# Hidden tiles turned only behind two-target products, and a down block's sums split in two

## The chip, the cores and the metric

One core of one Trainium2 chip runs the whole layer. The metric is the device time of one execution in microseconds (us); the runs of one kernel lie within a few tenths of a per cent of each other. Every time below comes from one profiled execution unless the text says that it is a median of runs.

## The reference, cut to what matters

The layer takes x of 256 tokens by 2048 columns in float32. It is a SwiGLU feed-forward network (FFN), a token mixer, and a second FFN, with RMS norms between:

```python
def swiglu_ffn(x, w_gate, w_up, w_down):              # 2048 -> 5632 -> 2048
    return (jax.nn.silu(x @ w_gate) * (x @ w_up)) @ w_down

x = x + 0.5 * swiglu_ffn(rms_norm(x, ffn1_norm), ...)
x = x + mixer(rms_norm(x, mix_norm))                  # Hawk recurrence beside a short gated convolution
x = x + 0.5 * swiglu_ffn(rms_norm(x, ffn2_norm), ...)
return rms_norm(x, final_norm)
```

The change touches only the two FFNs, and in them the step from `silu(gate) * up` to the product with `w_down`.

## The kernel before, in words

**Precision.** Every float32 weight tile is split on the chip into a rounded part `hi` (ScalarE, ACT: a cast) and the rest `lo` (VectorE, DVE: a subtraction), both in the format fp32r. A product sums hi·hi, hi·lo and lo·hi. One weight tile (`unit`) is 512 rows by 512 columns, 1 MB, held as 128 x 2048; its split costs two casts of 128 x 1024 and one DVE subtraction of 128 x 2048. The split parts rotate through three sets of buffers, so that the splitting runs about two products ahead of TensorE (PE) and no further.

**Two kinds of product.** `multiply` gets a list of targets (PSUM banks). With one target it issues 12 matmuls of 512 columns, with two targets 24. Inside `seven`, a 2 x 2 block product done in seven multiplications in place of eight (Strassen's scheme, in Winograd's form), the seven products have one target each and need a DVE sum or difference of weight tiles first; the up to four `usual` products between them have two targets. In `down`, the units of `add_units` have two targets, except the last ones of the last block. The order in `seven` is: product 0, product 4, usual, product 5, usual, product 6, product 2, usual, product 3, usual, product 1. The text speaks of them as p0, p4 and so on.

**Stages of an FFN.** The first 512 of the 5632 hidden columns are made plainly (unit 0). Then five rounds s = 0 to 4 follow, each a `seven` on `w_gate` and a `seven` on `w_up`, which give two more hidden units (1+2s and 2+2s) of 512 columns for both halves t = 0, 1 of the tokens. After rounds 0, 2 and 4 comes `down`, which multiplies the units made so far by `w_down`: for output columns 0 and 3 in units of two targets, and for columns 1 and 2 by a `seven` over the last two units m and n. In a down block with `others` the older units, the order is (0, others), (0, n), (3, others), (0, m), then the `seven`, then column 3 of n and m.

**Turning the hidden tiles.** A finished tile `h` has tokens on the partitions and must get its hidden columns there. `part` lets ACT sort the 2-byte halves of h into a buffer `plane` (two of them exist) and has SyncE (SP) issue a transposing DMA from `plane` back to h. `join` lets ACT sort the halves back into `plane`, cast them to the hi part of the big tile `hidden`, and lets DVE subtract for the lo part; in rounds 0, 2 and 4 (`again`) ACT also copies the float32 values to h once more. In the trace these are `COPY plane<-u_g`, `DMA_TRANSPOSE u_g<-plane`, `CAST h<-plane`, `TENSOR_TENSOR h<-plane,h` (with `z`, `s_g`, `sg` in the place of `u_g` for other tiles). A round finishes its four tiles in this order: unit 2+2s with t = 1 and t = 0 (after p6 and p2 of the up `seven`), unit 1+2s with t = 1 and t = 0 (before and after p1).

**When.** A tile is parted as soon as it is queued (`turn_hidden`, `begin_some`) when fewer than two are on the way. After every product of any kind the hook `onward` (in the list `after_product`) counts, joins the tile whose count has reached three, and starts another.

**The sums of a down block.** Its `seven` needs four sums of the float32 tiles of m and n, each split into hi and lo (`seven_of`; in the trace `hspare` and `hs`). `block_sums` makes them all after the unit (0, m) and ahead of the `seven`. The first sum, `spare`, is what p4 uses; `adds` and the rest give what p5, p6 and p2 use.

**What sets the order on an engine.** The kernel is written with a framework that plans the engines' queues while it builds the program. An instruction's place in the program text is its priority; where the planner reckons that its inputs or its buffer are not ready yet, it puts a later instruction that is ready in front. On the chip each engine then works through its own queue in that fixed order. Only `begin` and the end of the last block (`Engine.pinned`) are kept in program order.

Of the kernel before, what the change touches and what calls it, by code (L numbers as in the profile page):

```python
# [21 lines left out]
NT = S // P  # L22
KD = D // P
KF = FF // P
CW = 512
# [24 lines left out]
def hybrid_block(ctx: ExitStack, tc: tile.TileContext, a: dict, out: bass.AP):  # L50
# [35 lines left out]
    def f32(ap):  # L86
        return ap.bitcast(F32)
# [110 lines left out]
    after_product = []  # L198

    def multiply(targets, blk, apart=False, middle=None):  # L200


        more = dict(skip_group_check=True) if apart else {}
        for ps, st, begin, _ in targets:
            for j in range(UK):
                pe.matmul(ps, st[j][0], blk[j][0], start=begin and j == 0, stop=False, **more)
                pe.matmul(ps, st[j][1], blk[j][0], start=False, stop=False, **more)
        if middle:
            middle()
        for ps, st, _, end in targets:  # L210
            for j in range(UK):
                pe.matmul(ps, st[j][0], blk[j][1], start=False, stop=end and j == UK - 1, **more)
        for fn in after_product:
            fn()


    class Norm:
# [93 lines left out]
    def seven_of(sf, x0, x1, v, spare, parts, steps=None):  # L311

        a11, a12, a21, a22 = v[0, 0], v[0, 1], v[1, 0], v[1, 1]
        parts = iter(parts)

        def split(i, q):
            hi, lo = next(parts)
            act.copy(hi, q)  # L320
            dve.tensor_tensor(lo, q, f32(hi), op=ALU.subtract)
            sf[i] = [(hi[:, j, :], lo[:, j, :]) for j in range(UK)]

        sf.update({0: stationary(x0, 0), 1: stationary(x1, 0), 3: stationary(x1, 1)})
        dve.tensor_tensor(spare, a21, a22, op=ALU.add)
        split(4, spare)

        def adds():
            dve.tensor_tensor(a21, a11, a21, op=ALU.subtract)
            dve.tensor_tensor(a11, spare, a11, op=ALU.subtract)  # L330

        def rest():
            if steps is None:
                adds()
            split(5, a11)
            split(6, a21)
# [72 lines left out]
    def ffn(tag, norm, after, opening=False):  # L409
        with (  # L410
# [5 lines left out]
            wg, wu, wd = (a[f"ffn{tag}_w_{s}"][0] for s in ("gate", "up", "down"))  # L416
# [7 lines left out]
            hidden = {}  # L424
# [3 lines left out]
            tiles, moving = deque(), deque()  # L428

            def part(u, t, h, again):  # L430
                two = plane()
                act.copy(two.bitcast(U16).rearrange(flat, b=2), h.bitcast(U16).rearrange(mixed, b=2))
                nc.sync.dma_start(
                    h.bitcast(U16).rearrange("p (r c) -> p r c", c=P), two.bitcast(U16), transpose=True
                )
                return two
# [13 lines left out]

            def turn_hidden(*tile):
                tiles.append(tile)
                begin_some()

            def begin_some():
                while tiles and len(moving) < 2:
                    tile = tiles.popleft()
                    moving.append([0, tile, part(*tile)])

            def onward():  # L460

                for entry in moving:
                    entry[0] += 1
                while moving and moving[0][0] >= 3:
                    _, tile, two = moving.popleft()
                    join(two, *tile)
                begin_some()

            def on_the_way():
                return [*tiles, *(entry[1] for entry in moving)]  # L470

            after_product.append(onward)

            units, vs, sf, ready = [], {}, {}, []

# [200 lines left out]
            def down(last):  # L676
# [40 lines left out]

                def add(t, b, ps, tiles):
                    got[t, b] = [ps] + tiles
# [42 lines left out]
                if s % 2 == 0:  # L762
                    down(s == 4)
            extra.clear()
            after_product.clear()


    def small(name):
# [337 lines left out]
```

## Time and profile before

| | us |
|---|---|
| runs of the kernel | 1749.2, 1751.09, 1754.36 (median 1751.09) |
| the profiled execution, own time | 1749.34 |
| its span from first to last instruction | 1747.3 |
| PE busy in the span | 1710.1 |
| DVE busy | 1486.1 |
| ACT busy | 1137.4 |
| mean granted TensorE clock | 0.997 |

The span is 2.04 us shorter than the execution's own time; the rest lies around it. PE, the engine of the matmuls, is busy for all but 37.2 us of the span. DVE and ACT feed it: where a row shows PE idle, the row's bracket names the instruction of another engine that ended the wait. The names are those of the program with buffer numbers left out: `hi_d_p` and `lo_d_p` are the split parts for a one-target product of a down block's `seven`, `hi_d_x` those of a `usual` one, `raw_d` a weight tile (or, written by DVE, a difference of two), `s_d` a copy of a PSUM bank, `ps_d_c` the bank c of that `seven`; `g`, `u` in the place of `d` mean the gate and up products. Nearly all lines read L43, since one helper records every instruction; the groups are told apart by these names.

### The profile page before, as it was taken

To read this page: it belongs to the slowest core of one execution; us is meant where nothing else is said; L and a number is where in the kernel's file an instruction comes from. 1 tells how busy PE (TensorE), PEld (TensorE's weight loads), DVE (VectorE), ACT (ScalarE), POOL (GpSimd) and SP (SyncE) were. 2 spreads that over 40 slices of the span, in tenths; PEclk is the share of its full clock that TensorE was granted. 3 is DMA by queue.
4 is the path that set the end of the run, shared out by engine and by line. 5 is a ranking of instruction groups with operands and counts; after the bars stand their busy time and mean duration, and the time that the engine had idled before them with its cause. 6 is when DMAs were issued, how large, how long until landed. Compare 5 with 4: busy or idle time off the path is not lost. (4 is left out here: it accounts for less than half of the span.)

```text
span 1747.3 us, 20171 instructions
## 1 busy us (share of the span) xinstructions
PE 1710.1 (98%) x7859; PEld 1417.5 (81%) x7859; DVE 1486.1 (85%) x1233; ACT 1137.4 (65%) x1433; POOL 6.9 (0%) x32
## 2 busy tenths in 40 slices
PE   8999999999999999999999999999999999999998
PEld 6887887888887887888888887787787888878876
DVE  7998999989899888687987668989899888889876
ACT  6767567685567676666665456675567764676854
POOL 1000000000000000000000000000000000000000
PEclk9999999999999999999999999999999999999999
DMA  8566566695567674555556564595476656576852
GB/s 299 195 219 178 206 217 201 208 289 178 184 213 203 216 235 169 193 169 193 170 192 225 191 212 132 194 288 171 172 234 218 205 181 217 192 211 204 265 177 107
DMA packets 220383, 354.75 MB, mean 203 GB/s; under 512 B 52100, under 2 KB 54528, under 8 KB 220160
## 3 DMA queue, kind: packets, MB, share of 16 engines
q1 hardware_dynamic: 219824, 352.36, 62.0%
q8 instruction: 61, 1.00, 0.2%
q10 hardware_dynamic: 144, 1.05, 0.1%
q14 instruction: 34, 0.28, 0.0%
q0 software_dynamic: 320, 0.07, 0.0%
HBM read 339.82 MB, written 2.10 MB: 196 GB/s over the span
## 5 line engine op out<-in xcount | busy, mean ns | idle before, releaser
L43 DVE TENSOR_TENSOR lo_u_p<-raw_u,hi_u_p 128x2048 fp32r<-128x2048 f32 x70 | 159.2, 2286 | 24.4 <-ACT hi_u_p L43 23.9
L43 ACT CAST hi_u_p<-raw_u 128x1024 fp32r<-128x1024 f32 x140 | 141.1, 1047 | 55.5 <-DVE raw_u L43 23.5
L43 ACT CAST hi_g_p<-raw_g 128x1024 fp32r<-128x1024 f32 x132 | 132.9, 1047 | 65.5 <-DVE raw_g L43 40.0
L43 DVE TENSOR_TENSOR lo_g_p<-raw_g,hi_g_p 128x2048 fp32r<-128x2048 f32 x66 | 149.8, 2285 | 30.1 <-ACT hi_g_p L43 30.1
L43 PE MATMUL ps_d<-hi_d,h 128*128 128x512 f32 x704 | 167.2, 389 | 0.0
L43 PEld LDWEIGHTS ps_d<-hi_d,h 128*128 128x128 f32 x704 | 132.1, 188 | 27.4
L43 PE MATMUL ps_in<-xT_nm,hi_in 128*128 128x512 f32 x640 | 153.8, 391 | 0.0
L43 PEld LDWEIGHTS ps_in<-xT_nm,hi_in 128*128 128x128 f32 x640 | 117.2, 188 | 22.9 <-ACT tha L43 0.3
L43 ACT CAST hi_d_p<-raw_d 128x1024 fp32r<-128x1024 f32 x84 | 85.4, 1047 | 74.6 <-DVE raw_d L43 36.4
L43 ACT CAST hi_in<-raw_in 128x1024 fp32r<-128x1024 f32 x80 | 80.1, 1046 | 65.8 <-PE ps_in L43 42.8
L43 DVE TENSOR_TENSOR lo_in<-raw_in,hi_in 128x2048 fp32r<-128x2048 f32 x40 | 91.3, 2284 | 34.8 <-ACT hi_in L43 34.6
L43 DVE TENSOR_TENSOR lo_d<-raw_d,hi_d 128x2048 fp32r<-128x2048 f32 x44 | 100.7, 2289 | 21.1 <-ACT hi_d L43 19.8
L43 ACT CAST hi_u_x<-raw_u 128x1024 fp32r<-128x1024 f32 x80 | 80.4, 1047 | 42.8 <-PE ps_u_c L43 19.7
L43 DVE TENSOR_TENSOR lo_d_p<-raw_d,hi_d_p 128x2048 fp32r<-128x2048 f32 x42 | 95.5, 2285 | 9.3 <-ACT hi_d_p L43 9.2
L43 ACT CAST hi_d<-raw_d 128x1024 fp32r<-128x1024 f32 x88 | 87.9, 1045 | 21.1 <-PE ps_d_d L43 10.1
L43 DVE TENSOR_TENSOR raw_u<-raw_u,raw_u 128x2048 f32<-128x2048 f32 x40 | 91.6, 2290 | 9.6 <-DMA raw_u<-in_ffn_w_up_dram 8.9
L43 ACT CAST hi_g_x<-raw_g 128x1024 fp32r<-128x1024 f32 x80 | 80.2, 1046 | 25.6 <-PE ps_g_c L43 8.6
L43 DVE TENSOR_TENSOR lo_g_x<-raw_g,hi_g_x 128x2048 fp32r<-128x2048 f32 x40 | 91.3, 2284 | 1.6 <-ACT hi_g_x L43 1.5
L43 DVE TENSOR_TENSOR lo_u_x<-raw_u,hi_u_x 128x2048 fp32r<-128x2048 f32 x40 | 91.4, 2284 | 0.3
L43 DVE TENSOR_TENSOR raw_g<-raw_g,raw_g 128x2048 f32<-128x2048 f32 x37 | 84.5, 2285 | 6.0 <-DMA raw_g<-in_ffn_w_gate_dram 5.7
L43 PE MATMUL ps_d<-lo_d,h 128*128 128x512 f32 x352 | 87.3, 389 | 0.0
L43 PEld LDWEIGHTS ps_in<-xT_nm,lo_in 128*128 128x128 f32 x640 | 82.2, 191 | 3.2
(387 smaller groups left out, 3665.2 us busy)
## 6 DMA issues: line engine op xcount, KB each, us to landing
raw_d<-in_ffn_w_down_dram SPq DMA_DIRECT2D x88, 1024.0 KB, 5.6
raw_u<-in_ffn_w_up_dram SPq DMA_DIRECT2D x87, 1024.0 KB, 5.3
raw_g<-in_ffn_w_gate_dram SPq DMA_DIRECT2D x86, 1024.0 KB, 5.4
raw_in<-in_w_in_dram SPq DMA_DIRECT2D x40, 1024.0 KB, 5.1
raw_o<-in_w_out_dram SPq DMA_DIRECT2D x16, 1024.0 KB, 5.1
xres<-in_x_dram SPq DMA_DIRECT2D x4, 512.0 KB, 7.6
raw_u<-in_ffn_w_up_dram SPq DMA_DIRECT2D x2, 512.0 KB, 9.4
raw_g_first<-in_ffn_w_gate_dram SPq DMA_DIRECT2D x1, 1024.0 KB, 12.1
```

The costliest lines, as they stand in the source:

```text
L43: ins = getattr(self.engine, name)(*args, **kwargs)
```

## The change

The hook now runs only after a `multiply` with two targets, and at each such place it does one join and one part: it joins the tile that was parted at the place before, then parts the next in the queue. A tile isn't parted any more when it is queued, and at most one is on the way. Two-target products are the units of `add_units` (but not the very last, which are done one target at a time) and also the `usual` products inside `seven`.

In `down`, the first part of `seven_of` (`spare` and its split) now stands at the first unit after which no tile is on the way, which is ahead of the unit (0, m); the rest (`adds`, three splits, one more difference) stands inside the `seven`, after p4 and its bank copy and ahead of the first usual product.

```diff
-        for fn in after_product:
-            fn()
+        if len(targets) == NT:
+            for fn in after_plain:
+                fn()
...
             def turn_hidden(*tile):
                 tiles.append(tile)
-                begin_some()
-
-            def begin_some():
-                while tiles and len(moving) < 2:
+
+            def onward():
+
+                if moving:
+                    tile, two = moving.popleft()
+                    join(two, *tile)
+                if tiles:
                     tile = tiles.popleft()
-                    moving.append([0, tile, part(*tile)])
-
-            def onward():
-
-                for entry in moving:
-                    entry[0] += 1
-                while moving and moving[0][0] >= 3:
-                    _, tile, two = moving.popleft()
-                    join(two, *tile)
-                begin_some()
+                    moving.append((tile, part(*tile)))
...
-                sh, got = {}, {}
+                sh, got, rest = {}, {}, []
 
                 def block_sums():
-                    seven_of(
+                    return seven_of(
...
-                    )()
+                    )
...
-                for c, u in [(0, u) for u in others + [n]] + [(3, u) for u in others] + [(0, m)]:
+                for c, u in [(0, u) for u in others + [n]] + [(3, u) for u in others]:
                     add_units(c, [u])
-                block_sums()
+                    if not on_the_way() and not rest:
+                        rest.append(block_sums())
+                add_units(0, [m])
                 if tag == 1 and m == 5:
                     prepare()
-                seven(wd, (m, n), (2 * CW, CW), sh, [(u, hidden[u]) for u in others], f"d{tag}_{m}", keep, add)
+                seven(
+                    wd, (m, n), (2 * CW, CW), sh, [(u, hidden[u]) for u in others], f"d{tag}_{m}", keep, add,
+                    lambda i: rest.pop()() if rest else None,
+                )
```

Worked out from the two texts, a tile's places move like this. In rounds 1 and 3, which no down block follows, the second tile of unit 2+2s was joined after the third product behind its start, the fourth usual product of the up `seven`; it is now parted there and joined after the first usual product of the next gate `seven`. The two tiles of unit 1+2s were parted as soon as there was room; they are now parted after the first and second usual products of that gate `seven` and joined after the second and third. In rounds 0, 2 and 4 the down block's first three units take the places of those usual products; there the joins of the two tiles of unit 1+2s stand in the text where they stood before, after the second and the third unit.

More of the change, by code (lines that the diff above doesn't have):

```diff
@@ L196, in stationary @@
         return [(tile[:, j, t * P : (t + 1) * P], tile[:, j, S + t * P : S + (t + 1) * P]) for j in range(UK)]
-    after_product = []
+    after_plain = []
     def multiply(targets, blk, apart=False, middle=None):
@@ L452, in turn_hidden @@
                 tiles.append(tile)
-                begin_some()
-            def begin_some():
-                while tiles and len(moving) < 2:
-                    tile = tiles.popleft()
-                    moving.append([0, tile, part(*tile)])
-            def onward():
-                for entry in moving:
-                    entry[0] += 1
-                while moving and moving[0][0] >= 3:
-                    _, tile, two = moving.popleft()
-                    join(two, *tile)
-                begin_some()
+            def onward():
[3 more added lines that the diff above has]
+                if tiles:
+                    tile = tiles.popleft()
+                    moving.append((tile, part(*tile)))
             def on_the_way():
-                return [*tiles, *(entry[1] for entry in moving)]
-            after_product.append(onward)
+                return [*tiles, *(entry[0] for entry in moving)]
+            after_plain.append(onward)
             units, vs, sf, ready = [], {}, {}, []
@@ L764, in ffn @@
             extra.clear()
-            after_product.clear()
+            after_plain.clear()
     def small(name):
```

## The prediction

> **What bounds the kernel now.** I read the page's first part, then the chain of work that ended last, then the waits of PE, then the busy time by stretch, and last the timeline of one stretch of each kind.
>
> ```profile
> span 1747.3 us, 20171 instructions
> PE 1710.1 (98%) x7859; PEld 1417.5 (81%) x7859; DVE 1486.1 (85%) x1233; ACT 1137.4 (65%) x1433; POOL 6.9 (0%) x32
> ...
> 1259.82 5.44 PE ps_g_a L43 x24
> ...
> PE ps_d_c L43 <- ACT s_d L43: 4.5, 3, 3.0
> PE ps_d_c L43 <- DVE lo_d_p L43: 3.6, 2, 2.4
> ```
>
> PE is the bound: undisturbed it issues 24 matmuls in 5.44 us, 0.227 us each. The change removes no matmul, so all that it can win is PE's idle time, 1747.3 - 1710.1 = 37.2 us. The two longest waits say where much of that is: at the bank c of a down `seven`, that is at p4 and the first usual product; p4 is the first to need a weight difference. In the next table the difference between a stretch and its PE time is the idle time; the first six stretches are beginnings of gate `seven`s, the last six beginnings of down `seven`s.
>
> ```profile
> core 0: us, PE busy (x) PEld busy (x) DVE busy (x) ACT busy (x) POOL busy (x), PEclk, DMA share, GB/s
> 60.00:72.00 12.00, 11.35 (x49) 8.65 (x48) 11.19 (x9) 12.00 (x15) 0.00 (x0) 1.00 0.50 131
> 284.00:299.00 15.00, 13.44 (x58) 10.23 (x58) 14.30 (x12) 13.89 (x16) 0.00 (x0) 1.00 0.41 104
> 535.00:550.00 15.00, 12.68 (x53) 9.43 (x52) 13.28 (x11) 13.62 (x15) 0.00 (x0) 1.00 0.42 111
> 1084.00:1099.00 15.00, 13.06 (x55) 9.59 (x54) 12.86 (x10) 14.56 (x18) 0.00 (x0) 1.00 0.29 81
> 1302.00:1325.00 23.00, 20.81 (x90) 16.15 (x89) 18.78 (x14) 19.16 (x22) 0.00 (x0) 1.00 0.65 156
> 1556.00:1584.00 28.00, 24.90 (x107) 19.54 (x106) 23.41 (x16) 22.16 (x25) 0.00 (x0) 1.00 0.61 151
> 162.00:183.00 21.00, 18.58 (x81) 14.73 (x81) 21.00 (x13) 15.29 (x17) 0.00 (x0) 1.00 0.36 114
> 398.00:419.00 21.00, 21.00 (x94) 17.16 (x94) 20.62 (x28) 13.66 (x17) 0.00 (x0) 1.00 0.21 70
> 655.00:676.00 21.00, 19.70 (x87) 15.96 (x86) 16.86 (x10) 12.92 (x19) 0.00 (x0) 1.00 0.29 101
> 1182.00:1204.00 22.00, 20.53 (x90) 16.23 (x89) 22.00 (x17) 15.78 (x20) 0.00 (x0) 1.00 0.30 96
> 1430.00:1451.00 21.00, 20.80 (x92) 16.89 (x91) 17.53 (x10) 11.89 (x14) 0.00 (x0) 1.00 0.45 151
> 1682.00:1703.00 21.00, 18.01 (x72) 14.39 (x71) 17.05 (x12) 12.79 (x18) 0.00 (x0) 0.92 0.36 117
> ```
>
> Seams into rounds 2 and 4 (284, 535, 1302, 1556): 1.56 + 2.32 + 2.19 + 3.10 = 9.17 us. Round 0 (60, 1084): 0.65 + 1.94 = 2.59 us. Down `seven`s: 2.42 + 0 + 1.30 + 1.47 + 0.20 + 2.99 = 8.38 us. Together 20.1 us; the other 17 us are outside the reach of this change (start, end, mixer, other seams).
>
> **Term 1, the four seams.** One of them in full; the columns are start, duration, engine, and in brackets the idle time before and what ended it.
>
> ```profile
> 1552.60 0.37 SPq L168 DMA_DIRECT2D raw_g<-in_ffn_w_gate_dram  x1
> 1554.29 1.24 SPq L433 DMA_TRANSPOSE u_g<-plane  x1
> 1560.92 0.68 DVE L43 TENSOR_TENSOR z<-ps_u_a,z 128x512 f32<-128x512 f32 x1
> 1562.05 1.35 ACT L43 COPY plane<-u_g 128x1024 uint16<-128x1024 uint16 x1 [3.46 <-DMA u_g<-plane]
> 1563.96 1.04 ACT L43 COPY plane<-z 128x1024 uint16<-128x1024 uint16 x1
> 1564.08 0.69 DVE L43 TENSOR_TENSOR h<-plane,h 128x512 fp32r<-128x512 f32 x1 [2.48 <-ACT h L43]
> 1564.69 2.29 DVE L43 TENSOR_TENSOR raw_g<-raw_g,raw_g 128x2048 f32<-128x2048 f32 x1
> 1564.90 1.99 ACT L43 CAST hi_g_x<-raw_g 128x1024 fp32r<-128x1024 f32 x2
> 1567.01 1.99 ACT L43 CAST hi_g_p<-raw_g 128x1024 fp32r<-128x1024 f32 x2
> 1568.11 2.13 PE L43 MATMUL ps_g_c<-hi_g_p,xs 128*128 128x512 f32 x8 [1.54 <-ACT hi_g_p L43]
> ```
>
> The transposing DMA of the second tile lands at 1562.05, 7.8 us after it was issued. ACT stands 3.46 us before the join that it feeds, DVE 2.48 us before the join's subtraction, and only then come the weight difference for p4 (1564.69), its casts (1567.01) and PE, 1.54 us late; the rest of the stretch's 3.10 us follows behind it.
>
> After the change this join stands in the text behind the first usual product, and so behind the difference and the casts of p4; the next tile's part (1.04 us) likewise. What ACT has ready meanwhile is little, because the three sets of split buffers hold its casts back, so I leave the join in its place on ACT, with its wait. On DVE the difference is ready at 1560.92 + 0.68 = 1561.6, 3.1 us earlier than 1564.69, and is no longer behind the subtraction. On ACT the casts of p4 then start at 1563.96, where the part stood, or after the two casts of `hi_g_x` at 1565.95: 3.05 or 1.06 us earlier than 1567.01. PE's 1.54 us go to nothing or to 0.48, and what follows shrinks alike. Taken over the four seams, bounds 0 and -9.2: I take two thirds, **-6 us**, because the mechanism clears the first wait and part of the next. What is late next is the lo part of p4, on DVE.
>
> **Term 2, round 0.** The two tiles of unit 0 are turned while ACT is full (12.00 of 12.00 us, 14.56 of 15.00). Their parts move behind the first and second usual product. Bounds 0 and -2.6: **-1 us**.
>
> **Term 3, the down blocks.** In the first one:
>
> ```profile
> 160.47 0.68 DVE L43 TENSOR_TENSOR hs<-z,hs 128x512 fp32r<-128x512 f32 x1
> 163.28 0.68 DVE L43 TENSOR_TENSOR hs<-u_g,hs 128x512 fp32r<-128x512 f32 x1
> ...
> 167.28 2.28 DVE L43 TENSOR_TENSOR lo_d_p<-raw_d,hi_d_p 128x2048 fp32r<-128x2048 f32 x1
> 169.61 1.21 PE L43 MATMUL ps_d_c<-lo_d_p,hs 128*128 128x512 f32 x4 [2.42 <-DVE lo_d_p L43]
> ...
> 1687.22 1.05 ACT L43 CAST hi_d_p<-raw_d 128x1024 fp32r<-128x1024 f32 x1 [2.98 <-DVE raw_d L43]
> 1691.77 0.58 ACT L43 COPY s_d<-ps_d_c 128x512 f32<-128x512 f32 x1
> 1692.40 0.98 PE L43 MATMUL ps_d_c<-hi_d_x,h 128*128 128x512 f32 x3 [2.99 <-ACT s_d L43]
> ```
>
> PE waits 2.42 us for the lo part of p4, and DVE, which has no idle time in that stretch (21.00 of 21.00), has run two splits of the late sums before it, 2 x 0.68 = 1.36 us. They move behind p4, so the wait falls to 1.06 us, and in the second FFN's first block from 1.47 to 0.11. But they come back ahead of the first usual product and p5 on a full DVE, so of 2.7 us I keep -2.0. For the third block of the first FFN (1.30) I take -0.5. In the last block PE waits for the copy of bank c (1691.77), which on ACT stands behind a cast that waited 2.98 us for a difference on DVE. Four late-sum operations ahead of it there are 2.7 us; moved behind, the wait could fall to 0.3. With the clock's part below up to 4.3 us; the copy depends on several instructions in a row, so I take -2.5. The second blocks wait 0 and 0.20 and can't win. Sum **-5 us**, bounds 0 and -8.4 (-10 with the clock).
>
> ```profile
> 166.00:172.00 6.00, 3.58 (x16) 2.63 (x15) 6.00 (x6) 4.00 (x6) 0.00 (x0) 1.00 0.00 0
> 1692.00:1697.40 5.40, 5.00 (x15) 3.95 (x16) 4.12 (x2) 3.29 (x4) 0.00 (x0) 0.68 0.57 194
> ```
>
> After the wait of 2.99 us the granted clock is 0.68 for 5.4 us: PE is busy for 5.00 us with 15 matmuls that take 15 x 0.227 = 3.4 us elsewhere, 1.6 us lost on top. After the wait of 2.42 us it stayed at 1.00. So a wait cut to under 2.4 us saves these 1.6 us too. The Trainium skill ("TensorE: Matmul & The Clock Gate", Part 1: The HAM clock gate) puts the drop after an idle window of about 3.4 us that runs freely, not from the wait's start; the trace shows it after 2.99 us, so by that rule the 1.6 us would hang on the window's phase and could stay in the sum at any length.
>
> **Term 4, what is added: joins that wait.** No instruction is added; the same parts, transposing DMAs and joins are issued elsewhere.
>
> ```profile
> DMA to landing us min/median/max: 3.0/3.8/8.3
> ACT plane L43 <- DMA u_g<-plane: 13.9, 8, 3.5
> ACT plane L43 <- DMA s_g<-plane: 10.4, 6, 4.8
> ```
>
> In a down block a join now stands one unit (5.44 us of PE) behind its part, where three units, 16.3 us, lay between. A landing of 3.8 us fits, one of 8.3 doesn't; ACT then stands, and behind it the casts of the next unit, then DVE's subtraction, then PE once its lead of about two products is used up. On SP a transposing DMA that waits for its part holds back the 1 MB loads behind it; they are issued a product or more ahead, which hides about a microsecond. The fourteen waits above already cost ACT 24.3 us and PE not half of that. Bounds 0 and +6: **+2 us**, near the lower end, since most tiles still start when they are ready. A gain from this term is possible only through landings, and those are in the range.
>
> **Term 5, sums behind p4.** Four subtractions or splits on DVE and three casts on ACT now stand between p4 and p5, where bank copies and PE wait behind them. Where DVE has idle time ahead (17.53 busy of 21.00 in the stretch from 1430) they are done early and cost nothing; where it has none they cost up to 2.7 us a block. Bounds 0 and +8 (three full blocks): **+1 us**.
>
> Sum: -6 - 1 - 5 + 2 + 1 = **-9 us**. On the profiled execution's own 1749.34 us that is 1740.3; this lies 1.75 us under the median of the runs, 1751.09, so on the median 1742.
>
> **Rivals.** *The queues hardly change.* Priorities count only where two instructions are ready together. If ACT's queue keeps the join in its place and DVE's the small sums in the gaps where they are now, terms 1 and 2 are 0, term 3 a half (-2.5), the costs +2: 1750.6. For it speaks that ACT waited in the seam with nothing else ready, and that the landing isn't moved. The Trainium skill ("DMA: Bandwidth & Descriptors", Queues, rings and completion order) has SP's transfers in one ring on each DMA engine, taken in ring order, so a transposition stays behind the loads issued before it wherever it stands in the text; the trace agrees: that one was issued 1.69 us after a 1 MB load and took 7.8 us. Against it: the difference on DVE was ready 3.1 us before it ran.
>
> *The late sums starve p5 (slower).* Behind p4 DVE must do a usual product's lo part, a difference and the lo part of p5 (2.28 + 2.29 + 2.28) and the late sums, two `adds` and four more at 0.68 us: 10.9 us. PE's cover is p4 and the usual product, 36 x 0.227 = 8.2 us. That is a deficit of 2.7 us in each of six blocks, 16 us, against 10 us of p4's waits that go, and nothing won at the seams: +6 to +8, **1758 us**. It decides if DVE has done none of the late sums before p4. For it: DVE is full in two of the six stretches. Against: the tiles are joined well before that, and in the first block the sums were run in gaps.
>
> *A join behind each single unit (slower).* If the three tiles at a down block go strictly one after the other, each takes a part of 1.04, a landing and the join's first copy of 1.35: 6.2 us with a landing of 3.8, 10.7 with one of 8.3, against a unit's 5.44 of PE. One long landing in a block makes it 5.3 + 2 x 0.8 = 6.9 us late, of which PE's lead of two products hides 5.4. The 1.5 us left in six blocks are 9; with terms 1 and 2 at a half (-3.5) and term 3 at nothing it is about +5.5, 1757. It decides where landings of 7 us and more fall on these tiles, as the 7.8 us did in the seam; the median of 3.8 speaks against it.
>
> *All goes:* 20.1 + 1.6 = -21.7, 1729.4 us.
>
> **How the numbers follow.** A measurement of this kernel can tell about 0.3%, 5.3 us, from no change. The forecast has a chance of 0.50, in its own range of 1735 to 1748; 0.05 of it lies within 0.3%. All gone 0.06. Queues unchanged 0.20, all within. Sums starve p5 0.16, single-file joins 0.08; both slower. So faster 0.51, same 0.25, slower 0.24. The range reaches down to where the stalls are nearly all won, 1731, and up to the sums' case, 1758.
>
> **What would show it.** Right: in the seam's timeline the difference and casts of p4 stand ahead of the second join on DVE and ahead of the next part on ACT; PE busy in the four seam stretches rises by some 6 us in all; in the down stretches the waits for `lo_d_p` and `s_d` fall under 1 us and the clock row at the last block reads 1.00. Wrong: PE waits named for `hs` or for p5 (`ps_d_a` on `lo_d_p`), ACT waits on `plane` over 24 us with PE waits right behind them, or seams that read as before.

## The result, and the profile after

| | before | after |
|---|---|---|
| median of 5 runs, us | 1751.09 | 1741.21 |
| lowest and highest run, us | 1749.2 to 1754.36 | 1738.53 to 1744.24 |
| ratio of the times, 95% interval | | 0.9944, 0.9925 to 0.9962 |
| the profiled execution, own time, us | 1749.34 | 1740.98 |

The kernel is faster by 9.9 us. The forecast was 1742.0, and on the profiled execution 1740.3. The first lines of the page after:

```profile
span 1739.2 us, 20156 instructions
...
PE 1709.3 (98%) x7859; PEld 1416.1 (81%) x7859; DVE 1485.4 (85%) x1233; ACT 1135.1 (65%) x1433; POOL 6.9 (0%) x32
```

PE's work is the same, 1709.3 us against 1710.1; its idle time fell from 37.2 to 29.9 us. The waits after (sum, number, longest):

```profile
ACT plane L43 <- DMA u_g<-plane: 13.0, 7, 2.7
DVE h L43 <- ACT h L43: 12.6, 13, 3.5
ACT plane L43 <- DMA s_g<-plane: 10.4, 9, 5.1
ACT plane L43 <- DMA z<-plane: 8.1, 5, 2.9
...
PE ps_d_a L43 <- DVE lo_d_p L43: 3.2, 2, 1.6
...
PE ps_d_c L43 <- DVE lo_d_p L43: 0.2, 1, 0.2
```

PE's waits for the lo part at bank c (p4) fell from 3.6 to 0.2 us; those for the lo part at bank a (p5) rose from 0.3 to 3.2. ACT stands before joins for 31.5 us in all, longer than the 28.5 of before, while DVE's waits behind the joins (`h`) are down from 26.4 to 12.6. Next the busy time by stretch: two rounds 0, four seams into rounds 2 and 4, six down blocks. The stretches are laid alike in both kernels: a seam from 5 us before the first matmul of p4 to 17 after, a down block from 3 before to 18 after, round 0 from 3 to 18 us behind the first matmul of its gate `seven`.

```profile
61.00:76.00 15.00, 14.54 (x63) 11.22 (x62) 13.87 (x8) 14.80 (x18) 0.00 (x0) 1.00 0.60 175
1078.00:1093.00 15.00, 15.00 (x68) 12.18 (x67) 15.00 (x11) 13.12 (x17) 0.00 (x0) 1.00 0.72 176
286.00:308.00 22.00, 21.16 (x91) 16.14 (x90) 21.41 (x13) 20.14 (x24) 0.00 (x0) 1.00 0.49 139
536.00:558.00 22.00, 20.61 (x87) 15.68 (x87) 20.85 (x13) 20.08 (x24) 0.00 (x0) 1.00 0.51 146
1305.00:1327.00 22.00, 20.84 (x90) 15.94 (x89) 21.16 (x13) 20.19 (x24) 0.00 (x0) 1.00 0.49 141
1555.00:1577.00 22.00, 20.51 (x87) 15.66 (x86) 20.76 (x15) 20.53 (x23) 0.00 (x0) 1.00 0.53 161
162.00:183.00 21.00, 18.90 (x80) 14.20 (x79) 20.97 (x15) 16.80 (x20) 0.00 (x0) 1.00 0.35 106
404.00:425.00 21.00, 21.00 (x95) 17.16 (x94) 19.92 (x32) 14.90 (x20) 0.00 (x0) 1.00 0.47 160
654.00:675.00 21.00, 21.00 (x94) 17.40 (x93) 18.77 (x13) 15.17 (x22) 0.00 (x0) 1.00 0.35 116
1180.00:1201.00 21.00, 19.46 (x85) 15.63 (x85) 21.00 (x16) 14.57 (x19) 0.00 (x0) 1.00 0.41 136
1423.00:1444.00 21.00, 20.44 (x90) 16.60 (x90) 17.89 (x12) 14.22 (x18) 0.00 (x0) 1.00 0.45 150
1674.00:1695.00 21.00, 18.65 (x76) 14.93 (x75) 18.33 (x14) 13.74 (x20) 0.00 (x0) 0.92 0.36 118
```

The first number behind the length is PE's busy time; length less busy time is PE's idle time. Added up by kind, the same way for every kernel of this study (one profiled execution each):

| PE idle, us | rounds 0 | four seams | six down blocks | of these, first of FFN 1, first of FFN 2, last |
|---|---|---|---|---|
| before | 2.54 | 9.17 | 8.38 | 2.42, 1.47, 2.99 |
| after | 0.46 | 4.88 | 6.55 | 2.10, 1.54, 2.35 |
| hook_only | 0.42 | 3.98 | 7.40 | 4.00, 1.61, 1.18 |
| sums_only | 2.58 | 8.58 | 4.75 | 2.17, 1.27, 0.88 |
| unit0_only | 0.44 | 8.22 | 8.14 | 2.43, 1.41, 2.75 |
| unit0_at_once | 0.86 | 5.13 | 7.01 | 1.92, 1.61, 3.04 |
| every_product | 2.47 | 13.28 | 5.85 | 2.17, 2.28, 0.74 |
| two_in_flight | 0.44 | 0.93 | 7.25 | 1.95, 1.61, 3.69 |
| end_later | 0.45 | 6.07 | 6.13 | 2.38, 1.61, 1.73 |
| rest_split | 0.42 | 4.60 | 6.41 | 2.10, 1.86, 2.15 |
| two_end_later | 0.42 | 2.46 | 3.22 | 1.43, 1.59, 0.20 |
| rest_ahead | 0.39 | 4.99 | 5.06 | 2.02, 1.65, 1.39 |
| all_three | 0.39 | 2.02 | 5.33 | 1.78, 1.87, 1.68 |
| act_queue | 0.24 | 11.61 | 14.39 | 4.50, 5.07, 1.45 |

The names are those of the next section. These sums come from one execution each. The six kernels whose seams have the same program text (after, `hook_only`, `rest_ahead`, `unit0_at_once`, `end_later`, `rest_split`) differ there by 2 us, 3.98 to 6.07, so a smaller difference of one column is no finding.

From before to after the three columns give 2.08 + 4.29 + 1.83 = 8.2 us; the spans differ by 8.1. So the change of the profiled execution lies in the places that the prediction named, though not in its shares. The seam of the prediction, after:

```profile
1555.29 1.37 ACT L43 COPY plane<-u_g 128x1024 uint16<-128x1024 uint16 x1 [2.69 <-DMA u_g<-plane]
1555.54 2.28 DVE L43 TENSOR_TENSOR raw_g<-raw_g,raw_g 128x2048 f32<-128x2048 f32 x1
...
1557.74 0.68 DVE L43 TENSOR_TENSOR h<-plane,h 128x512 fp32r<-128x512 f32 x1
...
1559.11 1.99 ACT L43 CAST hi_g_p<-raw_g 128x1024 fp32r<-128x1024 f32 x2
...
1560.43 1.98 PE L43 MATMUL ps_g_c<-hi_g_p,xs 128*128 128x512 f32 x8
```

The join still stands 2.69 us for its landing, in the same place on ACT. But DVE makes the difference for p4 ahead of the join's subtraction, not behind it, and p4 starts with no idle time in its bracket, where it had 1.54.

The first down block after, and the last one:

```profile
167.01 1.20 PE L43 MATMUL ps_d_c<-lo_d_p,hs 128*128 128x512 f32 x4 [0.18 <-DVE lo_d_p L43]
...
173.08 2.28 DVE L43 TENSOR_TENSOR lo_d_p<-raw_d,hi_d_p 128x2048 fp32r<-128x2048 f32 x1
...
175.89 2.28 DVE L43 TENSOR_TENSOR lo_d_p<-raw_d,hi_d_p 128x2048 fp32r<-128x2048 f32 x1
...
178.22 1.21 PE L43 MATMUL ps_d_a<-lo_d_p,hs 128*128 128x512 f32 x4 [1.61 <-DVE lo_d_p L43]
...
1679.10 0.63 ACT L43 ACTIVATE junk_f<-xres 128x512 f32<-128x512 f32 x1 [3.48 <-DVE xres L43]
...
1683.65 0.58 ACT L43 COPY s_d<-ps_d_c 128x512 f32<-128x512 f32 x1
...
1684.28 3.08 PE L43 MATMUL ps_d_c<-hi_d_x,h 128*128 128x512 f32 x8 [2.35 <-ACT s_d L43]
```

At the first block the wait at p4 went from 2.42 to 0.18, and p5 waits 1.61 in its stead. At the last block PE still waits 2.35 us for the copy of bank c: ACT does the final norm's two squares (`junk_f`), the first after a wait of 3.48 us for `xres` on DVE, and three casts ahead of it.

The round 0 of the second FFN, before and then after:

```profile
1084.09 1.35 ACT L43 COPY plane<-sg 128x1024 uint16<-128x1024 uint16 x1 [1.98 <-DMA sg<-plane]
...
1086.25 0.58 ACT L43 COPY s_g<-ps_g_c 128x512 f32<-128x512 f32 x1
...
1086.88 2.11 PE L43 MATMUL ps_g_c<-hi_g_x,x 128*128 128x512 f32 x8 [1.81 <-ACT s_g L43]
```

```profile
1080.77 0.58 ACT L43 COPY s_g<-ps_g_c 128x512 f32<-128x512 f32 x1
...
1082.20 1.98 PE L43 MATMUL ps_g_c<-hi_g_x,x 128*128 128x512 f32 x8
```

Before, a join that waited 1.98 us held up the copy of bank c, and PE behind it 1.81 us. After, the copy runs ahead of both joins.

### The profile page after: what moved, and what is told of

Read it like the earlier page. It is cut to its first block, busy times and chain, and to the rows that moved or that the text cites. A ratio compares the mean times of both kernels' runs of the same rounds, so it can differ in the third digit from the quotient of the medians.

```text
span 1739.2 us, 20156 instructions
## 1 busy us (share of the span) xinstructions
PE 1709.3 (98%) x7859; PEld 1416.1 (81%) x7859; DVE 1485.4 (85%) x1233; ACT 1135.1 (65%) x1433; POOL 6.9 (0%) x32
```

## The experiments

Ratios are to the kernel before on the same chip (its medians there were 1751.37, 1752.25 and 1751.61 us), with 95% intervals; each kernel ran 4 to 11 times. Two ratios whose intervals overlap widely are not called different.

| kernel | median, us | ratio to before |
|---|---|---|
| hook_only | 1740.11 | 0.9938 [0.9926, 0.9950] |
| sums_only | 1747.27 | 0.9974 [0.9964, 0.9984] |
| rest_ahead | 1742.0 | 0.9944 [0.9928, 0.9961] |
| unit0_only | 1747.14 | 0.9970 [0.9958, 0.9982] |
| unit0_at_once | 1746.57 | 0.9973 [0.9959, 0.9987] |
| two_in_flight | 1737.65 | 0.9920 [0.9906, 0.9933] |
| act_queue | 1775.66 | 1.0132 [1.0114, 1.0149] |
| end_later | 1740.87 | 0.9928 [0.9915, 0.9940] |
| every_product | 1755.5 | 1.0023 [1.0009, 1.0037] |
| rest_split | 1745.47 | 0.9965 [0.9953, 0.9978] |
| two_end_later | 1732.49 | 0.9891 [0.9878, 0.9905] |
| all_three | 1735.7 | 0.9909 [0.9896, 0.9923] |

**Which half of the change?** `hook_only` has the new hook and the sums of before; `sums_only` has the old hook and the new sums, that is, only the last hunk of the change, from `sh, got, rest` on.

```diff
 # hook_only, against after
-                for c, u in [(0, u) for u in others + [n]] + [(3, u) for u in others]:
+                for c, u in [(0, u) for u in others + [n]] + [(3, u) for u in others] + [(0, m)]:
                     add_units(c, [u])
-                    if not on_the_way() and not rest:
-                        rest.append(block_sums())
-                add_units(0, [m])
+                block_sums()()
```

> The hook of the change alone; the down blocks' sums stand as in the kernel before. Theory (each part acts at its own place): the gains at the beginning of the second FFN's round 0 (about -2.9 us) and at the four seams (about -3.6 us) are here, the down blocks wait as before (p4's lo part 2.4 us in the first block, 1.5 in the fourth, 1.3 to 1.6 in the third): 1743 to 1745 us. Rival A (the sums carry it): the hook alone gives under 2 us, 1749 or more. Rival B (the two need each other, since late joins and sums share the queues): 1748 to 1751.

> The sums of the change alone; tiles are parted and joined as in the kernel before. Theory: only the down blocks change, p4's wait of 2.4 us in the first block goes and comes back as a wait of p5 of 1.5 to 2 us, the third block's 1.3 to 1.6 us go, the last falls by about half a microsecond: -1 to -3, 1748 to 1750 us. Rival A: this is the larger part, 1745 or less. Rival B: slower, 1752 or more, since p5 starves where the joins are not moved.

The hook alone is worth 11 us, the sums alone 4 to 5, both together 10: they do not add. The table of idle times says where. With the old hook the new sums take the down blocks from 8.38 to 4.75 us, the last one from 2.99 to 0.88; with the new hook only from 7.40 to 6.55: the first falls from 4.00 to 2.10, but the last goes the other way, from 1.18 to 2.35. The sums alone leave the seams nearly as they were (8.58 of 9.17).

**Where the late sums stand.** `rest_ahead` is the kernel after with the late sums put ahead of the `seven`, in place of behind p4.

```diff
                 add_units(0, [m])
+                rest.pop()()
```

> The change, but the late sums stand behind the unit (0, m) and ahead of the seven, so only the first sum is moved forward. Theory: in the first block p4's wait for its lo part comes back (over 1 us of the 2.4) and p5's wait of 1.6 us goes; nothing else moves; within 2 us of the changed kernel, 1740 to 1744. Rival (the place behind p4 is what helps the third block): the third block's 1.3 us come back too and the time is 2 to 4 us over the changed kernel's.

The same ratio as after. Most of the wait is back at p4, as in the kernel before, and about half of p5's stays:

```profile
PE ps_d_c L43 <- DVE lo_d_p L43: 3.4, 2, 2.0
...
PE ps_d_a L43 <- DVE lo_d_p L43: 1.5, 2, 1.2
```

Against 0.2 and 3.2 us after, and 3.6 and 0.3 before: putting the sums behind p4 moves a wait from p4 to p5 and is worth nothing that these runs can tell.

**Unit 0 and the rest of the hook.** `unit0_only` is the kernel before with only unit 0's two tiles turned behind two-target products; `unit0_at_once` is the kernel after with only these two tiles turned at once.

```diff
 # unit0_only, against before
             def turn_hidden(*tile):
+                if tile[0] == 0:
+                    late.append(tile)
+                    return
                 tiles.append(tile)
                 begin_some()
...
+                if plain and going:
+                    tile, two = going.popleft()
+                    join(two, *tile)
+                if plain and late:
+                    tile = late.popleft()
+                    going.append((tile, part(*tile)))
 # unit0_at_once, against after
             def turn_hidden(*tile):
-                tiles.append(tile)
+                if tile[0] == 0:
+                    early.append([0, tile, part(*tile)])
+                else:
+                    tiles.append(tile)
...
+                while early and early[0][0] >= 3:
+                    _, tile, two = early.popleft()
+                    join(two, *tile)
+                if not plain:
+                    return
```

> The kernel before, but the two tiles of unit 0 are parted and joined behind two-target products as in the change; all other tiles and the sums as before. Theory: in the second FFN's round 0 ACT copies bank c of the gate seven at once and PE's wait for that copy (1.8 us) and what follows it go, the first FFN's round 0 gains 0.3: 1747 to 1748.5 us, about -3. Rival (that gain comes from elsewhere, such as the landings): within 1 us of before.

> The changed kernel, but the two tiles of unit 0 are parted when they are queued and joined behind the third product, as before. The complement of the run that moved only these two. If the gain of the hook is a sum of places, the 2.9 us of round 0 of the second FFN come back and little else: 1744 to 1745 us, 3 to 4 above the changed kernel, with the four seams as in the changed kernel (about 8.6 us of lost PE time in all against 12.2 before). Rival: the tiles of unit 0 shift the whole first rounds, and the loss of the kernel before returns in other places too: 1747 or more. If the gains of single parts aren't additive here as they were not for the sums, it stays at 1741 to 1742.

These tiles, two in each FFN and four of 44 in all, seem to be worth about as much as the other 40: 0.30% alone, and 0.29% lost when they are taken out (0.9973 for 0.9944, with intervals that overlap). In the stretches of `unit0_only` one sees 2.1 us of it, at the rounds 0. In `unit0_at_once` this wait does not come back, against what was expected: its rounds 0 idle 0.86 us, not 2.54, with the old places of these tiles. Its profiled execution is 2.2 us longer than that of after (spans of 1741.4 and 1739.2); where the rest of the medians' difference lies stays open.

**The places, or one on the way?** The new hook does two things: it runs at two-target products only, and it keeps one tile on the way in place of two. `every_product` undoes the first, `two_in_flight` the second.

```diff
 # every_product
-        if len(targets) == NT:
-            for fn in after_plain:
-                fn()
+        for fn in after_plain:
+            fn()
 # two_in_flight
-                if moving:
-                    tile, two = moving.popleft()
+                for entry in moving:
+                    entry[0] += 1
+                while moving and moving[0][0] >= 2:
+                    _, tile, two = moving.popleft()
                     join(two, *tile)
-                if tiles:
+                while tiles and len(moving) < 2:
                     tile = tiles.popleft()
-                    moving.append((tile, part(*tile)))
+                    moving.append([0, tile, part(*tile)])
```

> The changed kernel, but the hook runs after every product, those with one target too; still one tile on the way, joined one place behind its part. It takes apart the two halves of the hook: the places (two-target products only) and the number on the way. Theory (the places bring the gain, because joins and parts stay out of the stretch of p0 and p4, where the first difference and its casts are due): the seams lose PE time as in the kernel before, about 12 us in the four against 8.6 in the changed kernel, round 0 of the second FFN loses its 2.9 us again, and a join stands one product of 2.7 us behind its part, so that ACT waits for landings more than the 31.5 us of the changed kernel: 1748 to 1753. Rival (one tile on the way in place of two is what helps): it stays near the changed kernel, 1740 to 1743.

> The changed kernel, but at each two-target product the tiles whose part lies two places back are joined and new ones are parted until two are on the way. It tests the cost that the prediction put at +2 us, joins that wait because only one place lies between. Theory: ACT's waits for the landings (31.5 us in all in the changed kernel) fall below 20 us, but PE did not stand behind them, so the time stays within 1.5 us of the changed kernel. Rival (the predicted term is real): the time falls by 2 to 4 us. Third: two tiles at once put two parts on ACT in one place, as before the change, and the seams lose again: 2 to 5 us slower.

At every product, one tile on the way is slower than the kernel before: without the places there is no gain. (Its joins also stand one product behind their parts, where the kernel before leaves three, so the number on the way is not all that differs from before.) One of its waits:

```profile
PE ps_g_c L43 <- ACT hi_g_p L43: 5.4, 5, 1.3
```

The seams lose 13.28 us, and here ACT's waits do reach PE: it waits for the very casts that stand behind the joins, at the gate's bank c 5.4 us.

With the places kept and two on the way, the seams are as good as closed:

```profile
1547.01 2.29 DVE L43 TENSOR_TENSOR lo_g_p<-raw_g,hi_g_p 128x2048 fp32r<-128x2048 f32 x1 [1.33 <-ACT hi_g_p L43]
...
1549.82 2.28 DVE L43 TENSOR_TENSOR raw_g<-raw_g,raw_g 128x2048 f32<-128x2048 f32 x1
```

In the kernel after, the lo part of p0 in that seam reads

```profile
1552.12 2.29 DVE L43 TENSOR_TENSOR lo_g_p<-raw_g,hi_g_p 128x2048 fp32r<-128x2048 f32 x1 [2.54 <-ACT hi_g_p L43]
```

There one join stands between the two casts of p0, so DVE is idle 2.54 us, and it has no time to spare later in the seam; with two on the way both casts come first, and DVE is idle 1.33. The difference for p4 then starts 6.7 us before p4 (1549.82 to 1556.5), where it was 4.9 (1555.54 to 1560.43). ACT's waits for the landings are 27.6 us, hardly less than 31.5: that they would fall under 20 was wrong. What the order of ACT's queue does to DVE matters here, not the sum of ACT's waits. On the time the rival has it, by which the predicted term is real: the ratio is about 4 us lower than that of after, but the intervals overlap, so the seams' rows carry this finding more than the times do.

**The landings.** `act_queue` lets ACT issue the transposing DMAs.

```diff
-                nc.sync.dma_start(
+                nc.scalar.dma_start(
                     h.bitcast(U16).rearrange("p (r c) -> p r c", c=P), two.bitcast(U16), transpose=True
```

> The changed kernel, but ACT issues the transposing DMAs from its own queue, in place of SP. Theory (the transposition waits in its queue behind the 1 MB load that SP issued some 1.7 us before): from issue to landing it takes 3 to 4 us in the odd seams too, where it takes 6.4 to 7.0 now, and ACT's waits for the landings fall from 31.5 us to under 12. Rival (the load takes the bandwidth, whatever the queue): the landings stay at 6 us and more. On the time: by the reading that PE no longer stands behind these waits, within 2 us of the changed kernel either way; if landings still set the pace in the seams, 3 to 5 us faster.

```profile
L434 ACTq DMA_TRANSPOSE u_g<-plane x20: 1247/1248/1532, 126.9 to 1672.1; - x20
...
DMA to landing us min/median/max: 3.0/4.7/10.3
```

In the kernel after the last row reads

```profile
DMA to landing us min/median/max: 3.0/4.0/7.0
```

Out of SP's queue the landings are no shorter, so the queue behind SP's loads is not what makes them long. The load itself does, as the trace shows when each landing is set beside that of the load issued just before it. In the kernel after, all ten transpositions issued up to 2.0 us behind a 1 MB load land 0.9 to 1.0 us after that load, whether this makes 4.3 us or 7.0; the long ones stand behind a load that itself landed late. Issued from ACT's queue, 20 of 22 such land 0.8 to 1.1 us after the load. The Trainium skill ("DMA: Bandwidth & Descriptors", Queues, rings and completion order) gives SP and ACT a ring each on the same 16 DMA engines, which take turns between rings; by that a load and a transposition share the engines from whichever queue they come, and the landings agree. Why a transposition ends behind the load and not beside it stays open. With that goes the prediction's reading that the queue's order kept the seam's transposition behind the load: it ends behind the load from another queue too. The price was elsewhere: each issue takes 1.25 us of ACT's queue, 44 of them 55 us, and the kernel became 23 us slower than before; PE idles 54.6 us in its execution, where it idled 29.9 after. Neither expectation on the time held.

**The last block.** `end_later` puts the final norm's first work behind column 1.

```diff
-                    if last:
+                    if end and c == 0:
+                        held_back.append(lambda: after(c, t))
+                    elif last:
                         after(c, t)
...
                     got[t, b] = [ps] + tiles
+                    while b == 0 and held_back:
+                        held_back.pop(0)()
...
-        if c == 0 and t == 0:
+        if "fin" not in held:
             held["fin"] = bigs.tile([P, D], F32, tag="big", name="fin")
```

> The changed kernel, but in the last down block the final norm's first work (the squares and products of output column 0) comes behind the products of column 1 in place of ahead of p5. Theory: the copy of bank c stood on ACT behind two squares (2 x 0.63 us and two reads of the accumulator) and a cast, so the wait of 2.35 us for it falls under 1 us, the granted clock stays at 1.00 there, and the block's lost PE time falls from 4.2 to about 1.5 us: 2 to 3 us faster than the changed kernel, about 1738.5. Rival: the casts of the late sums and of p5 hold the copy as long: no change. Second rival: the work comes back at the end, behind the last products, and what is won is given back there.

```profile
1682.20 1.05 ACT L43 CAST hi_d_p<-raw_d 128x1024 fp32r<-128x1024 f32 x1 [2.96 <-DVE raw_d L43]
...
1686.17 2.11 PE L43 MATMUL ps_d_c<-hi_d_x,h 128*128 128x512 f32 x8 [1.73 <-ACT s_d L43]
```

The squares are gone from ahead of the copy and the wait is 1.73, not under 1: the casts still stand there, behind one that waited 2.96 us for a difference on DVE. So the first theory holds in part and its rival in part. Against after the gain can't be told from nothing (0.9928 and 0.9944).

**p5's wait.** `rest_split` leaves behind p4 only what p5 needs of the late sums.

```diff
             split(5, a11)
+            return more
+
+        def more():
             split(6, a21)
...
-                    lambda i: rest.pop()() if rest else None,
+                    lambda i: rest.append(rest.pop()()) if i == 0 else rest.pop()() if i == 2 else None,
```

> The changed kernel, but of a down block's late sums only what p5 needs stands behind p4; the splits for p6 and p2 and the last difference stand behind p5. Theory: the waits for the lo part of p5 in the first blocks of each FFN (1.6 us each, with what follows 1.9 and 1.7) were the price of the late sums on a full DVE; they go under 0.5 us and nothing as long appears at p6 or p2, because the usual product between gives 5.4 us of cover: 2 to 3.5 us faster than the changed kernel. Rival: DVE is full for the whole block, so that the wait only moves on to p6 or p2, which the two splits now precede: the same time within 1 us.

```profile
159.01 4.62 DVE L43 TENSOR_TENSOR raw_d<-raw_d,raw_d 128x2048 f32<-128x2048 f32 x2
...
171.95 6.69 DVE L43 TENSOR_TENSOR lo_d_p<-raw_d,hi_d_p 128x2048 fp32r<-128x2048 f32 x3
...
176.49 1.20 PE L43 MATMUL ps_d_a<-lo_d_p,hs 128*128 128x512 f32 x4 [1.53 <-DVE lo_d_p L43]
...
179.89 1.40 PE L43 MATMUL ps_d_a<-hi_d_p,hs 128*128 128x512 f32 x5 [0.51 <-DVE hs L43]
```

Of the small sums only p5's own still stands ahead of p5's lo part on DVE, and PE waits 1.53 us for that part all the same; then 0.51 for the split that was moved, at p6. What stands ahead is another lo part: of the three that begin at 171.95, PE's wait ends with the second. In the built program, where the names have their numbers, it is that of p6:

```
lo_d1_1_p6_1419 <- raw_d1_1_11
lo_d1_1_p5_1394 <- raw_d1_1_10
```

p6's weight difference is the second of the two at 159.01, made ahead of p4's lo part, so p6's casts and its lo part are ready sooner than p5's, whose difference comes behind p4. The same order stands in the kernel after, at 173.08 (p6) and 175.89 (p5). So the planner's choice to put p6's lo part (2.28 us) before p5's is enough to account for the wait of 1.5 us, and the late sums are not what makes it. A kernel that turned these two round was not tried, so this cause is argued, not shown.

**Both finds together.**

> Two tiles on the way, each joined two two-target products behind its part, and the final norm's first work in the last block behind the products of column 1. If both gains are of separate places, the last block's lost PE time falls from 6.7 us to about 2 against the kernel with two on the way: 3 to 4.5 us faster than that one, 1733 to 1735. Rival: as the clock's fall is a matter of chance and not of this wait alone, only the wait itself is won, 1.5 to 2 us: about 1736.

> As the kernel with two on the way and the later final norm, and the late sums split as well. If the split of the sums takes the first blocks' waits for p5 (3.0 and 2.1 us of lost PE time with two on the way), it is 2 to 3.5 us faster than without it, about 1731; if the wait moves on to p6 or p2, no difference.

`two_end_later` is `two_in_flight` with the edit of `end_later`. It is the fastest of the study, 1732.49 us, 0.9891 [0.9878, 0.9905] of before and below both halves. The last block idles 0.20 us there; in `two_in_flight` it had idled 3.69. `all_three` adds the split of the sums and is not faster (0.9909), as `rest_split` by itself was not; its last block idles 1.68 us with the same later norm, so not all of the 3.5 us can be put down to that edit.

Nor are the seams closed for good. Of the 2.46 us in `two_end_later`'s seams 2.17 are one wait:

```profile
1549.94 1.35 ACT L43 COPY plane<-u_g 128x1024 uint16<-128x1024 uint16 x1 [4.00 <-DMA u_g<-plane]
...
1557.72 0.50 PE L43 MATMUL ps_g_c<-lo_g_p,xs 128*128 128x512 f32 x1 [2.17 <-DVE lo_g_p L43]
```

The landing took 8.5 us there, where the same tile took 6.3 in `two_in_flight`. ACT stood 4.00 us in place of 1.85, the casts of p4 came behind the join, and PE waited for p4's lo part. A long landing can still reach PE with two tiles on the way.

## Why the prediction was right, and where only its sum was

The forecast of -9 us met -9.9 on the medians; between the profiled executions it was -8.4. Two of the signs that the prediction named for being wrong turned up all the same, PE waits at p5 and ACT waits before joins of more than 24 us. And two of its signs for being right did not: the wait for `s_d` stayed at 2.35 us, and the clock row of the last block reads 0.92. By its steps:

- **Term 1, the seams, with term 4, joins that wait: -6 and +2, measured together 4.88 - 9.17 = -4.3.** The mechanism is the one described: ACT's join with its wait stayed, DVE's difference went ahead of the subtraction, p4's 1.54 us went. Both terms were sized too small by about the same: with two tiles on the way the seams reach 0.93 in one kernel and 2.46 and 2.02 in two others, so the new places are worth 6.7 to 8.2 us (the lower bound was 9.2), and one on the way costs 2.4 to 4.0 of them. Term 4 was right in sign and wrong in its working: it was to come in the down blocks from late landings; it came in the seams, from a join between two casts that DVE needed.
- **Term 2, round 0: -1, measured -2.1.** What was mis-sized is the hold-up: the join there kept a bank copy, and so PE, waiting; all of it went, not two fifths.
- **Term 3, down blocks, with term 5, late sums: -5 and +1, measured 6.55 - 8.38 = -1.8.** The wait at p4 fell as described (2.42 to 0.18, below the 1.06 forecast, since DVE's update of `xres`, 1.28 us, now comes behind p4's lo part too; the third block 1.30 to 0). But 1.6 us came back at p5 in each FFN's first block. The rival of late sums named this wait, but its mechanism is not the one that the runs show: the two `adds` and the last difference ran before p0 (154.68 to 156.82 in the first block), so that three splits and not six operations came behind p4, and with two of these moved on (`rest_split`) PE still waited 1.53 us. And the last block gave 0.64 instead of 2.5: the step that failed there is "moved behind, the wait could fall to 0.3". The four sums had not been what held the copy: in the kernel before they were over on DVE at 1675.4, 9 us before p4 began. The squares and the casts behind a late difference were; without the squares ahead (`end_later`) 1.73 us are left.
- **The step on the clock, 1.6 us within term 3, was wrong.** It said that a wait under 2.4 us saves the slow clock. After the wait of 2.35 us at 1684 the granted clock was 0.63:

```profile
1684.20:1688.80 4.60, 4.52 (x13) 3.60 (x14) 4.48 (x4) 3.42 (x6) 0.00 (x0) 0.63 0.44 170
```

Thirteen matmuls took 4.52 us of busy time in place of 2.95. The last section has what decides; the prediction's remark that the 1.6 us would hang on a window's phase comes closer to it than its limit of 2.4 us.

- **The rivals.** "The queues hardly change" is refuted by the seam's rows. "A join behind each single unit" had the right cause, one tile on the way, in the wrong place: up to 4 us in the seams in place of 9 in the down blocks. "All goes" was nearly within reach of the places, by `two_end_later`: 0.42 + 2.46 + 3.22 = 6.1 us of idle time left of 20.1.

So the sum was right by luck, because its errors cancel: seams and rounds 0 gave 1.4 us more than forecast after term 4, and the down blocks 2.2 us less.

What stays open: why the sums are worth 4 to 5 us with the old hook and nothing with the new one. Most of it lies in the last block: its wait falls by 2.11 us with the old hook (2.99 to 0.88) and grows by 1.17 with the new one (1.18 to 2.35), and the slow stretch of the clock behind it goes with it, about 1.6 us each way. Why the late sums turn that wait round, no run isolated.

## What to carry to other kernels

Where one engine prepares operands for another and both are nearly full, the place of a small chore in the queue is worth more than its wait: the same joins at one in flight made this kernel 0.6% faster behind the long products and 0.2% slower behind every product. Look in the trace not for the engine that waits longest, but for what is queued behind it that the bound engine needs next. And a sum that comes out right is no proof of its terms: only runs that undo one part at a time showed that half of this change was worth nothing measurable on top of the other.

## What the runs showed of the hardware

The clock does not fall at a fixed length of wait. At the p5 of the first down block the kernel after and `end_later` have the same stop of PE, 1.61 us, behind one matmul that had waited 0.3 us. The clock stayed in the first, as in `two_in_flight`, and fell in the other, and `end_later` differs from after only 1500 us later. The other way round, in `unit0_only` it stayed after a longer wait:

```profile
1688.56 1.66 PE L43 MATMUL ps_d_c<-hi_d_x,h 128*128 128x512 f32 x6 [2.75 <-ACT s_d L43]
```

What decides shows when an execution is cut into windows of 3.41 us. In all profiled executions a slow stretch lasts 3.41 us or twice that (only the one at an execution's end lasts longer, until past its last instruction), and within one execution the slow stretches begin a whole number of 3.41 us apart. So they fix where the windows lie. Here are the window with the stop of 1.61 us and the next one, first in the kernel after, then in `end_later`. PE's busy time is the first number behind the length, the granted clock the third number from the end:

```profile
176.46:179.88 3.42, 1.81 (x8) 1.38 (x8) 3.42 (x3) 2.18 (x3) 0.00 (x0) 1.00 0.95 300
179.88:183.29 3.41, 3.41 (x17) 2.69 (x16) 3.41 (x3) 2.84 (x4) 0.00 (x0) 1.00 0.29 52
```

```profile
175.81:179.22 3.41, 1.53 (x6) 0.86 (x5) 3.41 (x4) 2.17 (x3) 0.00 (x0) 1.00 0.71 207
179.22:182.63 3.41, 3.41 (x10) 2.63 (x9) 3.41 (x3) 1.70 (x3) 0.00 (x0) 0.50 0.34 115
```

In after PE idles 1.61 us of the first window, in `end_later` 1.88, because the wait of 0.3 us falls into the same window there. The 2.75 us of `unit0_only` lie across an edge, 1.37 us in one window and 1.38 in the next. Over the fourteen executions, between 100 and 1720 us, the clock fell sixteen times; in the window ahead of each fall PE had idled 1.76 to 3.11 us. In no window after which the clock stayed at 1.00 had it idled more than 1.73. So PE's idle time within one window decides, with the limit at about half of it. A slow window that PE fills costs it about 1.6 us.

The Trainium skill ("TensorE: Matmul & The Clock Gate", Part 1: The HAM clock gate) calls the window free-running and gives it a length of about 3.4 us: with that the traces agree. It has the clock fall after an idle window; here a window idle by about half was enough, and the measurement decides. Where the windows lie against a kernel's stops differs from one execution to the next. So a stop has a price that is partly a matter of chance, and removing a stop of 2 us can be worth 2 or nearly 4.
